# First norm's gain spread by TensorE from one row and read from PSUM, with the order of the first tiles' casts, low parts and transposes written down

## The chip, the cores and the metric

The kernel runs on one core of one Trainium2 chip. The metric is the device time of one execution in microseconds (us), as a median of runs. Five engines work side by side, each through its own list of instructions in order: TensorE (PE: matmuls and transposes, with its weight loads listed as PEld), VectorE (DVE), ScalarE (ACT), GpSimd (POOL) and SyncE (SP), which here only issues DMAs. ACT issues some DMAs too. An instruction starts when it is first in its engine's list and the semaphores it waits for have been raised.

## The reference

One layer of a hybrid encoder over 1024 positions with 1024 channels, all in float32:

```python
h = rmsnorm(x, g_mix[l])
z = h @ w_in[l]
...
y_pool = pool_mixer(u_pool, w_pool_grp[l], pool_scale[l])
...
y_attn = diff_attention(q, k, v, g_q[l], g_k[l], lam, g_sub[l], lambda_init)
gates = jax.nn.sigmoid(h @ w_gate[l] + b_gate[l])
merged = (gates[..., :D_MODEL] * (y_pool @ w_branch_pool[l])
          + gates[..., D_MODEL:] * (y_attn @ w_branch_attn[l]))
x = x + merged @ w_out[l]
h2 = rmsnorm(x, g_ffn[l])
x = x + jnp.square(jax.nn.relu(h2 @ w_up[l])) @ w_down[l]
```

The change touches the first line only: `rmsnorm` divides a row of x by the root of its mean square and multiplies it by the gain `g_mix`, one number for each channel.

## The kernel before

The 1024 positions are eight tiles t of 128 rows. For each, `norm_x(t)` calls `norm_transpose`: ACT squares the row and sums it (`Square`, with a second instruction that reads the sum out), DVE and POOL make the root `rs`, DVE multiplies x by `rs` and by the gain in two halves of 512 channels (`hn`), and PE transposes each half in four 128x128 blocks into one PSUM bank (`hps`). From the bank `split` makes two things, two blocks at a time: ACT casts a high part to the rounded type fp32r (`hT` with last index 0), and DVE subtracts that from the bank to leave a low part (index 1). Each tile so has four casts and four low parts, by pairs kp = 0 to 3 of channel blocks; two pairs share a bank. Tile 0 takes its sum of squares in two halves, on ACT and on DVE (`halves`).

The weights of a head (`rqkv`, eight blocks of 128 channels by 384 columns) are split the same way into `wqkv`, by ACT and by DVE or POOL. A product `z` of one tile and one head is `mm3` for eight blocks k: three matmuls each (high times high, high times low, low times high), 24 in all, into one of two PSUM banks. After z of a tile come the row norms of its q and k (`sq`, `ms`, `qn`), the V part, and the transposes `tk`; `qn` is read from the z bank, which is free for another tile only after that. All z of head 0 need the tiles' `hT`; the gates (`g`, with weights `fwgate`) need the `hT` too, and are filler work for PE, started by `gate_step`.

What sets the order: a scheduling layer takes the instructions in the order in which the program gives them priorities, models their times, and writes one list for each engine. `START` says in which order the first loads, splits and norms are given, `NX` in which step a tile's norm is given, `LX` in which step its x is loaded, `ORDER` how the stages of a step are interleaved. Nothing else holds one instruction behind another, except data and buffers, and a few explicit `issue_after`, the first of them at L793 for a unit of weights.

The gain is loaded by one broadcast DMA into all 128 partitions (`gmb`, 512 KB, L345), third on SP's queue behind the two halves of x0 and ahead of the eight weight loads and x1. PSUM has eight banks: two each for z, the scores (`sc`) and the transposes (`tr`), one for the output of attention (`ps_o`) and one for filler (`ps_f`). The last two are not used in the first steps.

## Time and profile before

| | us |
|---|---|
| median of 3 runs | 1529.36 (1529.09 to 1530.44) |
| the profiled execution | 1529.71 |
| its span in the trace | 1527.6 |
| TensorE busy in the span | 1509.7 |
| VectorE, ScalarE, GpSimd busy | 1048.5, 804.7, 319.8 |

The span runs from the first to the last traced instruction; 2.1 us of the profiled time lie around it. A row of a table of groups gives line, engine, operation, output and inputs, shapes and count, then busy us and mean ns, then the idle time of the engine ahead of the group and what ended it. A row of the timeline gives start, duration, engine and line, and in brackets the idle time before it with its releaser. A row of the table of waits gives the waiting engine and line, the releaser, the us in total, the number of times and the longest. The granted clock is a share of TensorE's full clock.

### The profile page before, as it was taken

What the parts mean: (1) busy time and instruction counts of PE and PEld (TensorE: products, weight loads), DVE (VectorE), ACT (ScalarE), POOL (GpSimd) and SP (SyncE); (2) the same over time, 40 slices, a digit from 0 to 9 for tenths busy, and PEclk for the clock granted to TensorE, in tenths of its full rate; (3) what the DMA queues carried; (4) which work ended last, traced back from release to release, by engine and by line L of the source; (5) the groups of instructions that cost most, each with busy time, mean ns of one, the idle gap of its engine ahead of it and who ended that gap; (6) DMA issues with size and microseconds to landing.
All of it is one profiled execution on the core that took longest, in us unless ns stands there. A gap on an engine that the chain in (4) does not pass through costs nothing.

```text
span 1527.6 us, 21675 instructions
## 1 busy us (share of the span) xinstructions
PE 1509.7 (99%) x7441; PEld 1302.0 (85%) x7441; DVE 1048.5 (69%) x2262; ACT 804.7 (53%) x1693; POOL 319.8 (21%) x412
## 2 busy tenths in 40 slices
PE   7999999999999999999999999999999999999998
PEld 6999999999898989888888888888888888888887
DVE  6776668777777777746578559766665668556572
ACT  6665556656565565454464466555555634333331
POOL 6687333335234242312100011000000000000000
PEclk9999999999999999999999999999999999999999
DMA  7253202112112131627365734554433799537750
GB/s 247 100 159 120 76 29 62 51 44 66 43 44 84 49 98 40 223 89 254 120 209 191 248 104 149 169 178 152 148 128 110 274 344 383 170 125 262 228 190 28
DMA packets 171608, 221.07 MB, mean 145 GB/s; under 512 B 10902, under 2 KB 104811, under 8 KB 171499
## 3 DMA queue, kind: packets, MB, share of 16 engines
q1 hardware_dynamic: 154090, 192.39, 38.0%
q10 hardware_dynamic: 17408, 27.30, 4.8%
q8 instruction: 59, 0.97, 0.3%
q14 instruction: 51, 0.41, 0.1%
HBM read 157.76 MB, written 61.90 MB: 144 GB/s over the span
## 4 chain that ended last, share of the span: by engine, by line
PE 95%; DVE 2%; DMA 1%; ACT 1%; SPq 1%; issue 0%; POOL 0%; DVEq 0%
PE z L126 6%; PE z L128 6%; PE z L127 6%; PE Da L126 4%; PE Da L128 4%; PE Da L127 4%; PE g L126 4%; PE g L127 4%; PE g L128 4%; PE Db L126 3%; PE Db L128 3%; PE Db L127 3%; PE X L128 3%; PE X L127 3%; PE X L126 3%; PE sc L484 2%
## 5 line engine op out<-in xcount | busy, mean ns | idle before, releaser
L126 PE MATMUL z<-wqkv,hT 128*128 128x384 f32 x512 | 174.9, 343 | 0.6 <-DVE qn L428 0.4
L128 PE MATMUL z<-wqkv,hT 128*128 128x384 f32 x512 | 173.7, 340 | 0.0
L127 PE MATMUL z<-wqkv,hT 128*128 128x384 f32 x512 | 173.5, 339 | 0.0
L495 ACT ACTIVATE s<-s,nm 128x256 f32<-128x256 f32 (+7 forms) x128 | 99.5, 778 | 46.5 <-DVE nm L487 45.6
L126 PE MATMUL g<-hT,fwgate 128*128 128x512 f32 x256 | 101.1, 395 | 0.1
L127 PE MATMUL g<-hT,fwgate 128*128 128x512 f32 x256 | 100.8, 394 | 0.0
L128 PE MATMUL g<-hT,fwgate 128*128 128x512 f32 x256 | 100.5, 393 | 0.0
L126 PEld LDWEIGHTS z<-wqkv,hT 128*128 128x128 f32 x512 | 96.8, 189 | 3.4 <-DVE qn L428 0.6
L127 PEld LDWEIGHTS z<-wqkv,hT 128*128 128x128 f32 x512 | 96.9, 189 | 3.1 <-POOL wqkv L121 0.2
L235 POOL TENSOR_TENSOR ms<-ms,mhalf 128x4 f32<-128x4 f32 x64 | 65.7, 1027 | 158.3 <-DVE ms L234 135.3
L128 PEld LDWEIGHTS z<-wqkv,hT 128*128 128x128 f32 x512 | 96.5, 189 | 2.5 <-DVE hT L121 0.3
L121 DVE TENSOR_TENSOR AT<-ta,AT 128x256 fp32r<-128x256 f32 (+1 forms) x160 | 62.2, 392 | 32.7 <-ACT AT L120 31.6
L487 DVE CUSTOM_DVE_ANT_0 s<-sc,dist 128x512 f32<-128x512 f32 (+3 forms) x128 | 73.9, 583 | 13.2 <-PE sc L485 12.1
L120 ACT CAST AT<-ta 128x256 fp32r<-128x256 f32 (+1 forms) x160 | 54.5, 347 | 37.9 <-PE ta L527 23.1
L484 PE MATMUL sc<-K,Q 128*128 128x512 f32 (+2 forms) x192 | 69.8, 365 | 0.5 <-DVE nm L487 0.5
L121 DVE TENSOR_TENSOR AS<-s,AS 128x512 fp32r<-128x512 f32 x64 | 44.1, 693 | 36.5 <-ACT AS L120 36.3
L485 PE MATMUL sc<-K,Q 128*128 128x512 f32 (+2 forms) x192 | 66.4, 350 | 0.0
L121 POOL TENSOR_TENSOR wqkv<-rqkv,wqkv 128x384 fp32r<-128x384 f32 x60 | 61.8, 1044 | 19.8 <-ACT wqkv L120 16.7
L121 POOL TENSOR_TENSOR fwgate<-frgate,fwgate 128x512 fp32r<-128x512 f32 x32 | 43.3, 1356 | 66.0 <-ACT fwgate L120 66.0
L126 PEld LDWEIGHTS g<-hT,fwgate 128*128 128x128 f32 x256 | 48.1, 188 | 9.3 <-ACT go L730 0.5
L128 PEld LDWEIGHTS g<-hT,fwgate 128*128 128x128 f32 x256 | 48.1, 188 | 8.9
L127 PEld LDWEIGHTS g<-hT,fwgate 128*128 128x128 f32 x256 | 48.1, 188 | 8.4
(455 smaller groups left out, 4485.0 us busy)
## 6 DMA issues: line engine op xcount, KB each, us to landing
wd<-in_w_down_dram SPq DMA_DIRECT2D x56, 512.0 KB, 5.6
wu<-in_w_up_dram SPq DMA_DIRECT2D x32, 512.0 KB, 4.4
udS<-us SPq DMA_DIRECT2D x64, 256.0 KB, 2.4
ur<-udS SPq DMA_DIRECT2D x32, 512.0 KB, 3.4
rqkv<-in_w_in_dram SPq DMA_DIRECT2D x64, 192.0 KB, 2.7
ud<-u ACTq DMA_DIRECT2D x48, 256.0 KB, 4.1
ur<-ud SPq DMA_DIRECT2D x24, 512.0 KB, 4.3
frgate<-in_w_gate_dram SPq DMA_DIRECT2D x32, 256.0 KB, 2.8
```

The source lines that it names most:

```text
L120: nc.scalar.copy(hi, src)
L121: return (lo_eng or nc.vector).tensor_tensor(lo, src, f(hi), op=ALU.subtract)
L126: nc.tensor.matmul(ps, lhs_hi, rhs_hi, start=first, stop=False, **kw)
L127: nc.tensor.matmul(ps, lhs_hi, rhs_lo, start=False, stop=False, **kw)
L128: nc.tensor.matmul(ps, lhs_lo, rhs_hi, start=False, stop=last, **kw)
L235: nc.gpsimd.tensor_tensor(dst, dst, mhalf[:, :n], op=ALU.pow)
L484: nc.tensor.matmul(dst, Q[:, i, 0, :], rhs, start=True, stop=False)
L485: nc.tensor.matmul(dst, Q[:, i, 1, :], rhs, start=False, stop=True)
L487: nc.vector.tensor_tensor_reduce(out=s[i][:, c : c + w], in0=sc[:, 0:w], in1=dist[:, o0 + c : o0 + c + w], scale=2.0 ** -(h + 1), scalar=B ...
L495: nc.scalar.activation(s[i][:, 0:n], s[i][:, 0:n], AF.Exp, bias=last, scale=-1.0, accum_out=Z[:, i, t : t + 1])
```

## The change

The gain comes as one row of 4 KB by a DMA on ACT's queue. PE multiplies a column of ones (one row of `ones`, so one contraction row) with each half of it, which puts the gain on all 128 partitions of two PSUM banks, those of `ps_o` and `ps_f`. The normalising products of tiles 0, 1 and 2 (`N_GP` = 3) read the gain from there; then ACT copies both banks to `gmb`, from which tiles 3 to 7 read it.

The rest is order. `in_turn` and `marks` chain a tile's casts one behind the other, and its low parts too. For tile 0 the weight splits are given between them by `split_more`, held behind the root of tile 0. The normalising product of a tile from t = 2 on is held behind the last low part of tile t-1. In z of tiles 1 to 6 the block k=4 is held behind the first half of the next tile's transposes, and k=6 behind the second. `small_params` is held behind tile 1's last low part, the first gate step behind tile 3's last cast. `START` and `NX` give tile 1's norm earlier.

```diff
--- before.py
+++ after.py
@@ -40,8 +40,8 @@
 PREP_AT = (2, 4, 6, 8)
 
 
-START = "x0 g n0 w0 w1 w2u w3u x1 s0p s1 x2 s2p s3 x3"
-NX = [-2, -1, 0, 0, 0, 1, 2, 3]
+START = "x0 g w0 w1 w2u w3u x1 n0 n1 x2 x3"
+NX = [-2, -2, 0, 0, 0, 1, 2, 3]
 LX = [-2, -2, -2, -2, 0, 0, 1, 1]
 FU = 170
 N_SC = 8
@@ -51,6 +51,7 @@
 ORDER = [(w[0], int(w[1:])) for w in O.split()]
 G_FIRST, G_Z = 9, 10
 LATE = 700
+N_GP = 3
 
 N_OP, N_E1, N_E2, N_R1, N_R2 = 8, 11, 6, 4, 3
 
@@ -115,10 +116,26 @@
     def f(ap):
         return ap.bitcast(F32)
 
+    marks = {}
+    begin = []
+
+    def in_turn(which):
+
+        behind = ExitStack()
+        if begin and which in marks:
+            behind.enter_context(tc.issue_after(marks[which]))
+        return behind
+
     def split(hi, lo, src, lo_eng=None):
 
-        nc.scalar.copy(hi, src)
-        return (lo_eng or nc.vector).tensor_tensor(lo, src, f(hi), op=ALU.subtract)
+        with in_turn("hi"):
+            marks["hi"] = nc.scalar.copy(hi, src).ins
+        if lo_eng is not None:
+            return lo_eng.tensor_tensor(lo, src, f(hi), op=ALU.subtract)
+        with in_turn("lo"):
+            lo_ins = nc.vector.tensor_tensor(lo, src, f(hi), op=ALU.subtract)
+            marks["lo"] = lo_ins.ins
+        return lo_ins
 
     def mm3(ps, lhs_hi, lhs_lo, rhs_hi, rhs_lo, first, last, more=False):
 
@@ -234,35 +251,50 @@
         nc.vector.tensor_scalar(dst, ss, c, EPS, op0=ALU.mult, op1=ALU.add)
         nc.gpsimd.tensor_tensor(dst, dst, mhalf[:, :n], op=ALU.pow)
 
-    def norm_transpose(xt, gb, t, dst, hn, small, banks, halves=False):
+    def norm_transpose(xt, gb, t, dst, hn, small, banks, halves=False, then=None):
 
         th, c0 = t // 4, (t % 4) * P
         ss = small.tile([P, 1], F32, tag="ss", name=f"ss{t}", bufs=2)
         rs = small.tile([P, 1], F32, tag="rs", name=f"rs{t}", bufs=2)
         if halves:
             s1 = small.tile([P, 1], F32, tag="ss1", name=f"ss1{t}")
-            nc.scalar.activation(hn[:, 0:512], xt[:, 0:512], AF.Square, accum_out=ss)
+            marks["hi"] = nc.scalar.activation(hn[:, 0:512], xt[:, 0:512], AF.Square, accum_out=ss).ins
             nc.vector.tensor_tensor_reduce(
                 out=hn[:, 512:D], in0=xt[:, 512:D], in1=xt[:, 512:D],
                 scale=1.0, scalar=D * EPS, op0=ALU.mult, op1=ALU.add, accum_out=s1,
             )
             nc.vector.tensor_scalar(rs, s1, ss, 1.0 / D, op0=ALU.add, op1=ALU.mult)
-            nc.gpsimd.tensor_tensor(rs, rs, mhalf[:, 0:1], op=ALU.pow)
+            marks["rs"] = nc.gpsimd.tensor_tensor(rs, rs, mhalf[:, 0:1], op=ALU.pow).ins
+            then(0)
         else:
-            nc.scalar.activation(hn, xt, AF.Square, accum_out=ss)
+            if t > 1:
+                marks.pop("hi")
+                marks.pop("lo")
+            with in_turn("hi"):
+                sq_ins = nc.scalar.activation(hn, xt, AF.Square, accum_out=ss).ins
+            if t == 1:
+                marks["hi"] = sq_ins
             rsq(rs, ss, 1, 1.0 / D)
         for j in range(2):
             js = slice(j * 512, (j + 1) * 512)
-            nc.vector.scalar_tensor_tensor(hn[:, js], xt[:, js], rs, gb[:, js], op0=ALU.mult, op1=ALU.mult)
+            with ExitStack() as behind:
+                if t >= 2:
+                    behind.enter_context(tc.issue_after(marks["hTlo", t - 1]))
+                nc.vector.scalar_tensor_tensor(hn[:, js], xt[:, js], rs, gb[j], op0=ALU.mult, op1=ALU.mult)
             trp, trtag = banks[j % len(banks)]
             ps = trp.tile([P, 512], F32, tag=trtag, name=f"hps{t}_{j}")
             for i in range(4):
                 k = 4 * j + i
-                nc.tensor.transpose(ps[:, i * P : (i + 1) * P], hn[:, k * P : (k + 1) * P], identf)
+                marks["hps", t, j] = nc.tensor.transpose(
+                    ps[:, i * P : (i + 1) * P], hn[:, k * P : (k + 1) * P], identf
+                ).ins
             for i in range(2):
                 kp = 2 * j + i
                 src = ps[:, i * 256 : (i + 1) * 256].rearrange("p (a b) -> p a b", a=2)
                 split(dst[kp, th, 0][:, :, c0 : c0 + P], dst[kp, th, 1][:, :, c0 : c0 + P], src)
+                marks["hT", t], marks["hTlo", t] = marks["hi"], marks["lo"]
+                if halves and kp in (1, 3):
+                    then(kp)
 
     def alloc_T(tile_fn, prefix, th):
         return {
@@ -313,6 +345,7 @@
             raws[h, kp] = rw
 
         def norm_x(t):
+            begin.append(t)
             if t % 4 == 0:
                 hT.update(alloc_T(htile, "hT", t // 4))
             if FU >> t & 1:
@@ -320,7 +353,12 @@
             else:
                 hn = ut([P, D], F32, f"hn{t}")
             banks = [(ps_t, "tr"), (ps_s, "sc")][: 2 if t < N_SC else 1]
-            norm_transpose(xs.pop(t), gmb, t, hT, hn, sp, banks, t == 0)
+            gb = g_ps if t < N_GP else [gmb[:, 0:512], gmb[:, 512:D]]
+            norm_transpose(xs.pop(t), gb, t, hT, hn, sp, banks, t == 0, lambda kp: split_more(kp))
+            begin.clear()
+            if t == N_GP - 1:
+                for j in range(2):
+                    nc.scalar.copy(gmb[:, j * 512 : (j + 1) * 512], g_ps[j])
 
         def split_w(h, kp, eng):
             rw = raws.pop((h, kp))
@@ -328,6 +366,11 @@
                 w = wt([P, 2, 384], f"wqkv{h}_{2 * kp + i}")
                 split(w[:, 0, :], w[:, 1, :], rw[:, i, :], eng)
                 Wh.setdefault(h, []).append(w)
+
+        def split_more(kp):
+            with tc.issue_after(marks["rs"]):
+                for p in {0: (0,), 1: (1,), 3: (2, 3)}[kp]:
+                    split_w(0, p, nc.vector if p % 2 else nc.gpsimd)
 
         KV = {}
         hT = {}
@@ -342,7 +385,11 @@
                 split_w(0, int(w[1]), nc.gpsimd if w[2:] else nc.vector)
             elif w[0] == "g":
                 gmb = ut([P, D], F32, "gmb")
-                nc.sync.dma_start(gmb, g_mix[0].partition_broadcast(P))
+                g_row = fu_tile("g_row")
+                nc.scalar.dma_start(g_row[0:1, :], g_mix)
+                g_ps = [pool.tile([P, 512], F32, tag=tag, name=f"g_ps{tag}") for pool, tag in ((ps_o, "o"), (ps_f, "f"))]
+                for j, ps in enumerate(g_ps):
+                    nc.tensor.matmul(ps, f(ones)[0:1, :], g_row[0:1, j * 512 : (j + 1) * 512], start=True, stop=True)
 
 
         rows = sp.tile([32, P], F32, name="rows")
@@ -411,7 +458,10 @@
                 l_hi = hT[k // 2, th, 0][:, k % 2, c0 : c0 + P]
                 l_lo = hT[k // 2, th, 1][:, k % 2, c0 : c0 + P]
                 w = Wh[h][k]
-                mm3(z[:, 0:384], l_hi, l_lo, w[:, 0, :], w[:, 1, :], k == 0, k == NK - 1)
+                with ExitStack() as behind:
+                    if h == 0 and 0 < t < NT - 1 and k in (4, 6):
+                        behind.enter_context(tc.issue_after(marks["hps", t + 1, k // 2 - 2]))
+                    mm3(z[:, 0:384], l_hi, l_lo, w[:, 0, :], w[:, 1, :], k == 0, k == NK - 1)
                 yield
 
         def stage_prep(h, t):
@@ -594,7 +644,8 @@
             nc.scalar.dma_start(r_dram[h].rearrange("(t q) -> t q", q=P), rT)
             yield
 
-        small_params()
+        with tc.issue_after(marks["hTlo", 1]):
+            small_params()
         N = H * NT
 
         def stage(w, g):
@@ -626,7 +677,7 @@
             for t in range(4, NT):
                 if LX[t] == g:
                     load_x(t)
-            for t in range(1, NT):
+            for t in range(2, NT):
                 if NX[t] == g:
                     norm_x(t)
             if g == G_DIST:
@@ -793,7 +844,9 @@
         with tc.issue_after(stored["lo"]):
             weight_unit(w_branch_attn, wa_dram, *units_left.pop(0))
 
-    for _ in range(G_FIRST):
+    with tc.issue_after(marks["hT", 3]):
+        gate_step()
+    for _ in range(G_FIRST - 1):
         gate_step()
     for g in range(4):
         for _ in pool_group(g):
```

Three places in the lists are spoken of in the prediction. In the rows, `hT_0_0` is a high part of tiles 0 to 3 and `hT_0_1` a low part (`hT_1_0` and `hT_1_1` for tiles 4 to 7), the number at the end of a name tells one buffer from another, and the brackets hold the semaphores that the instruction waits for, by the engine or DMA queue that raises them.

On ACT, from the first weight cast of the program to the first cast behind the transposes' second bank. Before:

```order
L120 CAST wqkv_0_200<-rqkv_0_186 128x384 [waits DMAHW3_49]
L120 CAST wqkv_1_203<-rqkv_0_186 128x384 [waits DMAHW4_49]
L120 CAST wqkv_2_206<-rqkv_1_189 128x384 [waits DMAHW5_49]
L120 CAST hT_0_0_150<-hps_0_167 128x2x128 [waits PE_49]
L120 CAST wqkv_3_209<-rqkv_1_189 128x384 [waits DMAHW6_49]
L120 CAST wqkv_4_214<-rqkv_2_192 128x384 [waits DMAHW7_49]
L120 CAST hT_0_0_154<-hps_1_177 128x2x128 [waits PE_49]
L120 CAST hT_0_0_152<-hps_0_167 128x2x128 [waits DVE_49]
```

And now:

```order
L132 CAST wqkv_0_185<-rqkv_0_155 128x384 [waits DMAHW3_49]
L132 CAST wqkv_1_188<-rqkv_0_155 128x384 [waits DMAHW4_49]
L132 CAST hT_0_0_169<-hps_0_192 128x2x128 [waits PE_49]
L132 CAST hT_0_0_171<-hps_0_192 128x2x128 [waits DVE_49]
L132 CAST wqkv_2_201<-rqkv_1_158 128x384 [waits DMAHW5_49]
L132 CAST wqkv_3_204<-rqkv_1_158 128x384 [waits DMAHW6_49]
L132 CAST hT_0_0_173<-hps_1_208 128x2x128 [waits PE_49]
L132 CAST hT_0_0_175<-hps_1_208 128x2x128 [waits DVE_49]
```

The third weight cast stood ahead of the first `hT` cast; now two weight casts stand ahead of two `hT` casts of the same bank, of which the second waits for DVE, and two more ahead of the other bank's. The weight casts of blocks 4 to 7 all stand behind.

On DVE, around the normalising product of tile 2 (`hn_278` before, `hn_283` now; tile 1's bank is `hps_0_255` and `hps_1_265` before, `hps_0_236` and `hps_1_246` now). Before:

```order
L376 SCALAR_TENSOR_TENSOR gg<-gqk 128x64 [waits DMAHW2_49,DMAHW1_49]
L379 TENSOR_TENSOR lp<-lqk 128x128 [waits DMAHW3_49]
L234 TENSOR_SCALAR ms_0_432<-ms_0_432 128x4 [waits DVE_49]
L121 TENSOR_TENSOR hT_0_1_151<-hps_0_255,hT_0_0_150 128x2x128 [waits Activation_49]
L256 SCALAR_TENSOR_TENSOR hn_278<-x_212,rs_280,gmb 128x512 [waits DMAHW4_49,Pool_49]
L256 SCALAR_TENSOR_TENSOR hn_278<-x_212,rs_280,gmb 128x512
```

And now:

```order
L136 TENSOR_TENSOR hT_0_1_170<-hps_0_236,hT_0_0_169 128x2x128 [waits Activation_49]
L251 TENSOR_SCALAR rs_313<-ss_312 128x1 [waits Activation_49]
L136 TENSOR_TENSOR hT_0_1_172<-hps_0_236,hT_0_0_171 128x2x128 [waits Activation_49]
L136 TENSOR_TENSOR hT_0_1_174<-hps_1_246,hT_0_0_173 128x2x128 [waits PE_49,Activation_49]
L136 TENSOR_TENSOR hT_0_1_176<-hps_1_246,hT_0_0_175 128x2x128 [waits Activation_49]
L423 SCALAR_TENSOR_TENSOR gg<-gqk 128x64 [waits DMAHW2_49,DMAHW1_49]
L426 TENSOR_TENSOR lp<-lqk 128x128 [waits DMAHW3_49]
L283 SCALAR_TENSOR_TENSOR hn_283<-x_255,rs_285,g_pso 128x512 [waits DMAHW4_49,Pool_49]
L283 SCALAR_TENSOR_TENSOR hn_283<-x_255,rs_285,g_psf 128x512
```

The product of tile 2 stood behind one low part of tile 1; now it stands behind all four, and behind `gg` and `lp`.

On PE, the transposes of tiles 5 and 6 (`hn_401` and `hn_467` before, `hn_408` and `hn_474` now). Before, ahead of and in z of tile 3:

```order
L126 MATMUL z_3_597<-wqkv_1_203,hT_0_0_150 128x384
L261 MATMUL hps_0_408<-identf,hn_401 128x128 [waits DVE_49,PE_49]
L261 MATMUL hps_0_408<-identf,hn_401 128x128 x3
L127 MATMUL z_3_597<-wqkv_1_203,hT_0_0_150 128x384
L261 MATMUL hps_1_418<-identf,hn_401 128x128 [waits DVE_49,PE_49]
L261 MATMUL hps_1_418<-identf,hn_401 128x128 x3
L128 MATMUL z_3_597<-wqkv_1_203,hT_0_1_151 128x384
L126 MATMUL z_3_597<-wqkv_2_206,hT_0_0_152 128x384
L261 MATMUL hps_0_474<-identf,hn_467 128x128 [waits DVE_49,PE_49,Activation_49]
L261 MATMUL hps_0_474<-identf,hn_467 128x128 x3
L127 MATMUL z_3_597<-wqkv_2_206,hT_0_0_152 128x384
```

And now, behind z of tile 3 and 22 gate products:

```order
L288 MATMUL hps_0_415<-identf,hn_408 128x128 [waits DVE_49,PE_49]
L288 MATMUL hps_0_415<-identf,hn_408 128x128 x3
L288 MATMUL hps_1_425<-identf,hn_408 128x128 [waits DVE_49,PE_49]
L288 MATMUL hps_1_425<-identf,hn_408 128x128 x3
L288 MATMUL hps_0_481<-identf,hn_474 128x128 [waits DVE_49,PE_49]
L288 MATMUL hps_0_481<-identf,hn_474 128x128 x3
L418 MATMUL cols_ps<-identf,rows 128x32 [waits DMAHW6_49,DMAHW7_49,DMAHW0_49,PE_49]
L288 MATMUL hps_1_491<-identf,hn_474 128x128 [waits DVE_49]
L288 MATMUL hps_1_491<-identf,hn_474 128x128 x3
L496 MATMUL tk_0_515<-identf,qn_0_446 128x128 [waits DVE_49]
L496 MATMUL tk_0_515<-identf,qn_0_446 128x128
L143 MATMUL z_4_671<-wqkv_0_185,hT_1_0_337 128x384 [waits DVE_49,Activation_49]
```

The transposes of both tiles lay among the products of z of tile 3, with 18 of those still behind them; now they stand behind all of them and behind each other, and z of tile 4 follows. The product `hn_474` stands on DVE behind the last low part of tile 5:

```order
L136 TENSOR_TENSOR hT_1_1_342<-hps_1_425,hT_1_0_341 128x2x128 [waits PE_49,Activation_49]
L136 TENSOR_TENSOR hT_1_1_344<-hps_1_425,hT_1_0_343 128x2x128 [waits Activation_49]
L283 SCALAR_TENSOR_TENSOR hn_474<-x_404,rs_476,gmb 128x512 [waits DMAHW6_49,Pool_49]
L283 SCALAR_TENSOR_TENSOR hn_474<-x_404,rs_476,gmb 128x512
L419 COPY cols<-cols_ps 128x24 [waits PE_49]
L420 TENSOR_SCALAR gs<-cols 128x1 [waits DVE_49]
L136 TENSOR_TENSOR hT_1_1_338<-hps_0_481,hT_1_0_337 128x2x128 [waits Activation_49]
L136 TENSOR_TENSOR hT_1_1_340<-hps_0_481,hT_1_0_339 128x2x128 [waits Activation_49]
L478 TENSOR_TENSOR qn_2_584<-z_2_525,ms_2_577 128x2x2x64 [waits PE_49,Pool_49]
```

And `qn_2`, which frees the bank for z of tile 4, stands behind two low parts of tile 6 (`hps_0_481`), where before it stood behind `cols`, with tile 6's low parts all ahead of it and taken from banks filled during z of tile 3.

## Prediction

> **What bounds the kernel now.** I read the page's busy table first, then TensorE's table of waits, then the chain that ended last.

> ```profile
> PE 1509.7 (99%) x7441; PEld 1302.0 (85%) x7441; DVE 1048.5 (69%) x2262; ACT 804.7 (53%) x1693; POOL 319.8 (21%) x412
> PE hps L261 <- DVE hn L256: 10.6, 2, 8.8
> PE X L128 <- DVE A L121: 0.9, 1, 0.9
> 8.97 5.76 DMA x<-in_x_dram
> 16.17 0.57 POOL rs L235
> 16.76 0.76 DVE hn L256
> 17.66 1.30 PE hps L261 x8
> ```

> TensorE (PE) works in 1509.7 of 1527.6 us; it is idle for 17.9. Of these, 10.6 are two waits of the first transposes for a normalised tile (8.8 before tile 0, 1.8 before tile 1); the next entry is 0.9. So nothing outside the first 19 us is to be won by a better order, but every new idle microsecond of PE is a microsecond of the result. The last four rows are the chain before tile 1: the DMA of x1, its row sum and root, the normalising product, the transposes.

> The stage table adds a cost that no table of waits counts. Its columns are the stretch, its length, busy time (with counts) of PE, weight loads, DVE, ACT and POOL, then the granted clock.

> ```profile
> 16.00:18.00 2.00, 0.34 (x3) 0.37 (x4) 1.32 (x3) 1.42 (x3) 0.56 (x1) 1.00 0.75 185
> 18.00:20.00 2.00, 2.00 (x11) 1.62 (x10) 2.00 (x9) 1.37 (x3) 1.55 (x3) 0.67 0.80 289
> 20.00:22.00 2.00, 2.00 (x9) 1.90 (x8) 1.78 (x7) 1.96 (x7) 1.92 (x3) 0.50 0.79 232
> 22.00:24.00 2.00, 2.00 (x14) 1.96 (x14) 2.00 (x7) 1.80 (x5) 1.93 (x4) 0.97 1.13 338
> ```

> After the idle time in 16 to 18, PE is busy at a clock of 0.67, 0.50 and 0.97: lost are 2 x (0.33 + 0.50 + 0.03) = 1.7 us.

> **The start.** These are timeline rows: start, duration, engine, operation, and the idle time before.

> ```profile
> 0.72 1.28 ACT L244 ACT_TABLE_LOAD   x1 [0.72 <-PEq L1514]
> 3.57 0.63 ACT L244 ACTIVATE hn<-x 128x512 f32<-128x512 f32 x1 [1.57 <-DMA x<-in_x_dram]
> 5.40 0.57 POOL L250 TENSOR_TENSOR rs<-rs,mhalf 128x1 f32<-128x1 f32 x1 [3.16 <-DVE rs L249]
> 7.95 1.41 DVE L256 SCALAR_TENSOR_TENSOR hn<-x,rs,gmb 128x512 f32<-128x512 f32 x2 [2.70 <-DMA gmb<-in_g_mix_dram]
> 8.75 1.97 PE L261 MATMUL hps<-identf,hn 128*128 128x128 f32 x8 [8.75 <-DVE hn L256]
> 9.06 5.07 POOL L121 TENSOR_TENSOR wqkv<-rqkv,wqkv 128x384 fp32r<-128x384 f32 x4 [3.08 <-DMA rqkv<-in_w_in_dram]
> 9.99 0.37 ACT L120 CAST hT<-hps 128x256 fp32r<-128x256 f32 x1
> 10.41 0.69 PE L126 MATMUL z<-wqkv,hT 128*128 128x384 f32 x1
> 12.78 0.53 ACT L120 CAST wqkv<-rqkv 128x384 fp32r<-128x384 f32 x1
> 14.75 1.06 ACT L252 ACTIVATE hn<-x 128x1024 f32<-128x1024 f32 x1 [1.44 <-DMA x<-in_x_dram]
> 15.52 0.34 PE L128 MATMUL z<-wqkv,hT 128*128 128x384 f32 x1
> 17.66 1.30 PE L261 MATMUL hps<-identf,hn 128*128 128x128 f32 x8 [1.80 <-DVE hn L256]
> 18.33 0.37 ACT L120 CAST hT<-hps 128x256 fp32r<-128x256 f32 x1 [0.85 <-PE hps L261]
> 18.75 0.69 PE L126 MATMUL z<-wqkv,hT 128*128 128x384 f32 x1
> ```

> The root for tile 0 is there at 5.97, but the product starts at 7.95, when the broadcast gain has landed. With the gain in PSUM the product can start near 6.0, 1.95 earlier, and the first z product at 10.41 - 1.95 = 8.5. What the gain costs now:

> ```profile
> gmb<-in_g_mix_dram SPq DMA_DIRECT2D x1, 512.0 KB, 6.2
> x<-in_x_dram SPq DMA_DIRECT2D x2, 256.0 KB, 3.0
> ```

> The 512 KB leave SP's queue, so the weights and x1 behind them come earlier; I take the 2 to 3 us by which a smaller load of this table lands sooner (3.0 against 6.2). The new row goes out first on ACT's queue at about 0.7, ahead of the table load, whose delay is covered: ACT sat idle for 1.57 before its first square. By the 3.0 of the x halves the row lands near 4. The two 512-column products are not in the trace. [...]

> Does z_0's end come earlier? ACT now casts w0, w1, the first two hT groups, w2, w3, two hT groups, then w4 to w7. From 8.0 (9.99 - 1.95), four hT casts of 0.37, two waits of some 0.4 for the DVE part of the same bank, and six weight casts of 0.53 end at 8.0 + 1.5 + 0.8 + 3.2 = 13.5, not before 13.31 as now (12.78 + 0.53). POOL's low part of w5 comes two of its 1.27 (5.07 over 4) after w4's cast at 11.9: 14.5, and eight products are behind it. So z_0 ends near 15.9 as now (15.52 + 0.34): the 1.95 is **not kept**. What is kept: x1 no longer sets its square (14.75). ACT is free at 13.5, so the chain from square to transposes, 17.66 - 14.75 = 2.9, ends at 16.4, with PE idle for about 0.5 instead of 1.8. z_1 starts **1.3 earlier**, and such a short gap should not bring the half clock: another **1.7**. Start: -3.0; bounds -5.0 (all of 1.95 kept too) and +3.4.

> **The new waits.** Their prices, by group (busy us, mean ns), are:

> ```profile
> L121 DVE TENSOR_TENSOR hT<-hps,hT 128x256 fp32r<-128x256 f32 x32 | 12.4, 415 | 0.3
> L120 ACT CAST hT<-hps 128x256 fp32r<-128x256 f32 x32 | 11.0, 374 | 4.3 <-PE hps L261 3.8 <-DVE hT L121 0.2
> L252 ACT ACTIVATE hn<-x 128x1024 f32<-128x1024 f32 x7 | 7.4, 1062 | 1.8 <-DMA x<-in_x_dram 1.8
> L252 ACT ACTIVATION_READ_ACCUMULATOR hn<-x 128x1 f32 x7 | 1.3, 191 | 0.0
> L730 ACT ACTIVATE go<-g,cols 128x512 f32<-128x512 f32 x2 | 1.4, 688 | 1.4 <-DVE cols L372 1.4
> L366 ACT ACTIVATE dist<-di 128x1024 f32<-128x1024 int32 x1 | 1.1, 1064 | 0.0
> L120 ACT CAST fwgate<-frgate 128x512 fp32r<-128x512 f32 x6 | 3.7, 618 | 1.0 <-DMA frgate<-in_w_gate_dram 1.0
> L423 ACT ACTIVATE sq<-z 128x256 f32<-128x256 f32 x5 | 1.9, 377 | 3.0 <-PE z L128 3.0
> L120 ACT CAST V<-z 128x128 fp32r<-128x128 f32 x5 | 1.3, 261 | 0.0
> L428 DVE TENSOR_TENSOR qn<-z,ms 128x256 f32<-128x256 f32 x5 | 2.1, 420 | 1.5 <-PE tk L446 1.3 <-POOL ms L235 0.2
> ```

> A cast is 0.37, a low part 0.42, a row square 1.06 + 0.19 = 1.25, half a normalising product 0.70 (1.41 over 2). The first cast follows the first transpose by 0.67 (18.33 - 17.66). z products at full clock go at a pitch of 0.17:

> ```profile
> 46.50 0.33 PE L128 MATMUL z<-wqkv,hT 128*128 128x384 f32 x1
> 46.67 0.33 PE L126 MATMUL z<-wqkv,hT 128*128 128x384 f32 x1
> 44.48 0.19 PEld L126 LDWEIGHTS z<-wqkv,hT 128*128 128x128 f32 x1 [0.32 <-DVE qn L428]
> ```

> *Transposes of tile 2.* The product hn2 stands on DVE behind the last low part of tile 1 (and two small products, of which I take 0.5, under a low part's 0.42 each), where before it stood behind the first. From the first transpose of tile 1: cast at 0.67 to 1.04, the square of tile 3 to 2.29, casts two and three to 3.0, the fourth behind its bank's low part to 3.9, low part 4.3, small products 4.8, hn2 5.5. PE starts z_1 at 1.1 (18.75 - 17.66), has six products, waits 0.6 for cast two (2.66) and its low part, does six more until 3.8, and reaches the transposes written in ahead of k=4: idle 1.7. Sum **+2.3**.

> *Tile 3.* Behind hn2 ACT has the first copy of the gain (by the 0.69 of a 512-column read), a square 1.25, a V cast and the first hT cast, then the other copy 0.69, dist 1.06, and three casts around sq and V of z_1: with sq 0.38 and V 0.26 each, and cast pairs that overlap a little, some 6.0 to the last cast's end, and 0.42 + 0.70 more to hn3: 7.1. PE holds 24 products at 0.17 and eight transposes at 0.14 (18.75 - 17.66 over 8) in this time, 5.2. **+1.9**, part of it before z_2's k=2, part at the transposes.

> *Gate.* The first gate step is held behind tile 3's last cast, and its weight cast (0.62) stands behind two squares (2.5) and that cast; PE comes to it 5.1 after tile 3's first transpose, the cast is done at 6.3. **+1.0** (bounds 0 and 1.3).

> *Tiles 5 and 6.* This is the largest. On PE the transposes of tile 6 now follow those of tile 5 **with nothing between**, and hn6 stands on DVE behind the last low part of tile 5; before, both lay among products of z_3, and hn6 waited for nothing of tile 5. From the first transpose of tile 5: cast until 1.04, square of tile 7 until 2.29, casts two and three until 3.0, low part 3.5, cast four 3.9, low part 4.3, hn6 5.0. PE's eight transposes take 1.1: idle **3.9**. Then z_4 waits, as in the last row above (0.32), for qn_2, since it reuses z_2's bank; but qn_2 now stands behind the low parts of tile 6, that is behind transposes (0.67), cast 0.37, go 0.69, cast 0.37, low part 0.42, qn 0.42: 2.9 after tile 6's first transpose, while PE has 1.3 of transposes. **+1.6**, less the old 0.3.

> *Clock.* A gap of 1.8 cost 1.7 above; gaps of 1.7, about 1 and 3.9 are new. I count one more drop at about half its price, since a part of the slow stretch falls into z_4's wait: +0.9; bounds 0 and three times 1.7.

> *At nothing:* the rest of the program. The same work stands there in a slightly other order up to the middle and in the same order behind it; PE's largest single wait there is the 0.9 quoted first, so I give it 0, with 2 on either side. The two copies of the gain are in the sum for tile 3; nothing else waits for them, since tile 3's product is the first to read the copy.

> **Sum.** -3.0 + 2.3 + 1.9 + 1.0 + 3.9 + 1.3 + 0.9 = +8.3 against the profiled 1529.71 (span 1527.6 and 2.1 around it): 1538.0. That run lies 0.35 above the median of 1529.36, so I say **1537.7**.

> **A rule beside it.** The row of 16 to 18 shows that 1.8 us of idle PE sufficed for a half clock of about 3.4 us. [...] By the row, all three gaps may: +5.1 in place of 0.9, 1541.9. [...]

> **Rivals.**
> - *The gain holds* (faster). The 1.95 of the start, the 1.3 at tile 1 and the 1.7 of the clock stay, and the handed-down orders cost under 2, because casts overlap (the pitch of a cast pair is under its duration) and hn6 is ready when tile 5's transposes end. 1529.4 - 5 + 2 = 1526 or down to 1524. For it: TensorE's only large waits are removed. Against: hn6 cannot start before the last low part of tile 5. It decides once the tile 6 gap is under 1. Chance 0.13.
> - *It washes out.* The start gives 4 to 5 and tile 6 costs 4, the other waits 1 or 2: 1527 to 1532. Decided by the bank waits in z_0. Chance 0.17.
> - *The gain arrives late*: the f32 row products take several microseconds, and hn starts at 8 or later. Since z_0 is tied to POOL and ACT anyway, up to 2 us are free; it gives the forecast plus 0 to 3, 1538 to 1541. Included in slower, 0.1.
> - *Clock drops at every gap*: 1542. Included in slower, 0.12.
> - The forecast and its near surroundings (1533 to 1541): 0.48.

> Faster by over 0.2% is below 1526.3, slower above 1532.4; a measurement of this kernel can tell about that much from no change. Chances: faster 0.13, same 0.17, slower 0.70. The range reaches from 1528 (leaving out the gain and a piece of the wash-out) to 1543 (the drops at every gap).

> **What would show it.** Right: hn of tile 0 near 6.0; z_0 still ending near 15.9; x1's square released by ACT's own order and not by a DMA; in TensorE's table of waits, hps <- DVE hn over 15 us in all with three or more entries, the longest after the start near 4, between 40 and 55 us; z <- DVE qn near 1.5; clock 1.00 in 18 to 22. Wrong: z_0 ending before 14.5, or no gap over 2 us between the transposes of tiles 5 and 6. After 70 us the two orders cost the same; a difference there would be a cause that I don't have.

## The result and the profile after

The changed kernel takes 1539.27 us (median of 5 runs, 1539.01 to 1540.83), the kernel before beside it 1529.56: a ratio of 1.0066 with a 95% interval of 1.0055 to 1.0078. It is **slower by 9.7 us**. The span of its profiled execution is 1537.2 us, 9.6 more than before.

These are the busy row of the page and TensorE's table of waits of the changed kernel (engine and line, releaser, us in total, times, longest):

```profile
PE 1516.6 (99%) x7445; PEld 1304.4 (85%) x7445; DVE 1047.8 (68%) x2262; ACT 807.8 (53%) x1695; POOL 318.8 (21%) x412
PE hps L288 <- DVE hn L283: 6.7, 5, 3.9
PE g_pso L392 <- DMA g_row<-in_g_mix_dram: 2.7, 1, 2.7
PE sc L534 <- DVE nm L537: 1.5, 1, 1.5
PE z L144 <- POOL wqkv L134: 1.1, 2, 0.6
PE z L143 <- ACT K L503: 0.8, 1, 0.8
PE g L143 <- ACT fwgate L132: 0.6, 1, 0.6
```

The wait of 8.8 us for the first transposes is gone from the table. Of it, 2.1 us are the earlier start (the transposes begin at 6.67 instead of 8.75); the rest is there still, as the wait of 2.7 for the gain's row and as the time in which TensorE spreads the gain. What is new is the row of 3.9 among the five of `hps`. The timeline of the changed kernel shows the start and the waits that follow:

```profile
2.73 2.04 PE L392 MATMUL g_pso<-g_row,ones 1*128 1x512 f32 x2 [2.73 <-DMA g_row<-in_g_mix_dram]
4.57 1.91 PE L392 MATMUL g_psf<-g_row,ones 1*128 1x512 f32 x2
5.87 0.75 DVE L283 SCALAR_TENSOR_TENSOR hn<-x,rs,g_pso 128x512 f32<-128x512 f32 x1 [0.76 <-POOL rs L267]
8.29 0.67 PE L143 MATMUL z<-wqkv,hT 128*128 128x384 f32 x1
15.44 0.34 PE L145 MATMUL z<-wqkv,hT 128*128 128x384 f32 x1
16.09 1.23 PE L288 MATMUL hps<-identf,hn 128*128 128x128 f32 x8 [0.31 <-DVE hn L283]
17.18 0.44 PE L143 MATMUL z<-wqkv,hT 128*128 128x384 f32 x1
21.60 0.63 PE L288 MATMUL hps<-identf,hn 128*128 128x128 f32 x4 [1.31 <-DVE hn L283]
27.88 0.63 PE L288 MATMUL hps<-identf,hn 128*128 128x128 f32 x4 [1.02 <-DVE hn L283]
33.76 0.50 PE L143 MATMUL g<-hT,fwgate 128*128 128x512 f32 x1 [0.63 <-ACT fwgate L132]
47.29 0.63 PE L288 MATMUL hps<-identf,hn 128*128 128x128 f32 x4 [3.90 <-DVE hn L283]
50.23 0.66 PE L143 MATMUL z<-wqkv,hT 128*128 128x384 f32 x1 [0.84 <-ACT K L503]
```

The first product of tile 0 starts at 8.29 instead of 10.41, but its last is issued at 15.44 against 15.52: two microseconds are lost on the way. z of tile 1 starts at 17.18, 1.57 earlier than before. By 50 us that is paid back several times. These rows show the path that the long wait follows, from the transposes of tile 5 to the normalising product of tile 6:

```profile
42.36 1.03 PE L288 MATMUL hps<-identf,hn 128*128 128x128 f32 x8
43.43 1.06 ACT L274 ACTIVATE hn<-x 128x1024 f32<-128x1024 f32 x1
45.66 0.37 ACT L132 CAST hT<-hps 128x256 fp32r<-128x256 f32 x1 [0.55 <-DVE hT L136]
46.06 0.42 DVE L136 TENSOR_TENSOR hT<-hps,hT 128x256 fp32r<-128x256 f32 x1 [0.44 <-ACT hT L132]
46.40 1.40 DVE L283 SCALAR_TENSOR_TENSOR hn<-x,rs,gmb 128x512 f32<-128x512 f32 x2
```

ACT squares tile 7 between the casts of tile 5; the last low part ends at 46.48, and `hn` of tile 6 starts with it. The stretches of two microseconds behind the long wait show the clock (third column from the end):

```profile
46.00:48.00 2.00, 0.71 (x5) 0.55 (x5) 1.75 (x3) 0.08 (x2) 0.00 (x0) 1.00 0.00 0
48.00:50.00 2.00, 1.39 (x7) 0.97 (x6) 1.34 (x5) 1.78 (x5) 0.00 (x0) 0.56 0.03 10
50.00:52.00 2.00, 1.77 (x6) 1.80 (x7) 1.94 (x6) 0.97 (x3) 0.46 (x1) 0.50 0.31 121
52.00:54.00 2.00, 2.00 (x8) 2.00 (x7) 1.49 (x3) 0.36 (x1) 0.00 (x0) 0.50 0.00 0
54.00:56.00 2.00, 2.00 (x10) 2.00 (x9) 0.00 (x0) 0.00 (x0) 0.00 (x0) 0.73 0.00 0
```

After the gap the clock is at half for some 7 us (48.25 to 55.07), in which TensorE is busy but for 0.84. Busy time times the missing share is 1.39 x 0.44 + 1.77 x 0.5 + 2 x 0.5 + 2 x 0.27 = 3.0 us.

### The profile page after: what moved, and what is told of

Same layout as the page of the kernel before. It is cut to its first block, busy times and chain, and to the rows that moved or that the text cites. A ratio compares the mean times of both kernels' runs of the same rounds, so it can differ in the third digit from the quotient of the medians.

```text
span 1537.2 us, 21688 instructions
## 1 busy us (share of the span) xinstructions
PE 1516.6 (99%) x7445; PEld 1304.4 (85%) x7445; DVE 1047.8 (68%) x2262; ACT 807.8 (53%) x1695; POOL 318.8 (21%) x412
## 4 chain that ended last, share of the span: by engine, by line
PE 91%; DVE 4%; DMA 2%; ACT 2%; issue 1%; POOL 1%; SPq 0%; ACTq 0%; DVEq 0%; POOLq 0%
PE z L143 5%; PE z L144 5%; PE z L145 5%; PE Da L143 4%; PE Da L145 4%; PE Da L144 4%; PE g L143 3%; PE g L144 3%; PE g L145 3%; PE Db L145 3%; PE Db L143 3%; PE Db L144 3%; PE X L145 3%; PE X L144 3%; PE X L143 3%; PE sc L534 2%
## 5 line engine op out<-in xcount | busy, mean ns | idle before, releaser
L252 POOL TENSOR_TENSOR ms<-ms,mhalf 128x4 f32<-128x4 f32 x64 | 66.0, 1032 | 138.6 <-DVE ms L251 134.6
L537 DVE CUSTOM_DVE_ANT_0 s<-sc,dist 128x512 f32<-128x512 f32 (+3 forms) x128 | 74.3, 584 | 14.4 <-PE sc L535 13.5
L484 POOL TENSOR_TENSOR qn<-qn,ggh 128x128 f32<-128x128 f32 x64 | 32.8, 514 | 107.6 <-DVE qn L478 82.0
## 6 DMA issues: line engine op xcount, KB each, us to landing
wd<-in_w_down_dram SPq DMA_DIRECT2D x56, 512.0 KB, 5.1
wu<-in_w_up_dram SPq DMA_DIRECT2D x32, 512.0 KB, 4.8
udS<-us SPq DMA_DIRECT2D x64, 256.0 KB, 2.3
ur<-udS SPq DMA_DIRECT2D x32, 512.0 KB, 3.5
ud<-u ACTq DMA_DIRECT2D x48, 256.0 KB, 3.8
ur<-ud SPq DMA_DIRECT2D x24, 512.0 KB, 6.7
frgate<-in_w_gate_dram SPq DMA_DIRECT2D x32, 256.0 KB, 2.6
```

The source lines that it names most:

```text
L252: nc.gpsimd.tensor_tensor(dst, dst, mhalf[:, :n], op=ALU.pow)
L484: nc.gpsimd.tensor_tensor(qn[:, :, 1, :], qn[:, :, 1, :], ggh.unsqueeze(1).broadcast_to([P, 2, HD]), op=ALU.mult)
L537: nc.vector.tensor_tensor_reduce(out=s[i][:, c : c + w], in0=sc[:, 0:w], in1=dist[:, o0 + c : o0 + c + w], scale=2.0 ** -(h + 1), scalar=B ...
```

## The experiments

My theory: the hold of a tile's normalising product behind the last low part of the tile before makes the waits, and the waits pull the clock down. The rivals: the gain itself costs (products on TensorE, copies on ACT, reads from PSUM); or the chains of casts, or the held gate step, cost. "Before" stands for the kernel before, run beside each group on the same chip.

### The gain alone

The kernel before, with the gain's row, its two products, `N_GP` = 3 and the two copies, and nothing of the order:

```diff
-                nc.sync.dma_start(gmb, g_mix[0].partition_broadcast(P))
+                g_row = fu_tile("g_row")
+                nc.scalar.dma_start(g_row[0:1, :], g_mix)
...
+                    nc.tensor.matmul(ps, f(ones)[0:1, :], g_row[0:1, j * 512 : (j + 1) * 512], start=True, stop=True)
```

> The kernel before with the gain alone: one row, two TensorE products into the banks of ps_o and ps_f, tiles 0 to 2 read it from PSUM, then two copies to gmb; no order is written down. If the loss of the change is its order (my reading), this keeps the earlier start and loses nothing big: 1526 to 1530, ratio 0.998 to 1.000, no wait of the transposes over 2 us after the start. If the PSUM gain itself costs (products on TensorE, copies on ACT, reads from PSUM), it is 1532 or more.

Measured: 1531.99, ratio 1.0020 (1.0010 to 1.0029). It falls between the two expectations, at the edge of the second: slower than before, though nothing is held. Rows of the timeline of its profiled execution (1534.29, so 2.3 over the median):

```profile
17.36 0.59 ACT L328 COPY gmb<-g_pso 128x512 f32<-128x512 f32 x1
18.19 1.08 ACT L253 ACTIVATE hn<-x 128x1024 f32<-128x1024 f32 x1
19.25 1.06 ACT L253 ACTIVATE hn<-x 128x1024 f32<-128x1024 f32 x1
20.54 0.61 ACT L328 COPY gmb<-g_psf 128x512 f32<-128x512 f32 x1
21.92 0.69 PE L127 MATMUL z<-wqkv,hT 128*128 128x384 f32 x1 [2.14 <-ACT hT L121]
```

Since x and the gain come earlier, ACT's list now has both copies and two squares between the casts of tile 1, and TensorE waits 2.14 us for a cast; the clock is at half from 21.59 to 25.00. A further wait of 3.0 us lies far behind, where `ta` waits for `s`. So an earlier start was worth nothing by itself here: the work moves, and ACT becomes the engine that is waited for. The two copies (0.59 and 0.61) belong to the gain and stand ahead of the awaited cast, so the rival that the gain itself costs is in part borne out; how much of the 2.2 us is theirs was not separated. That is why an order was worth writing down at all.

### The order alone

The changed kernel with the broadcast DMA back in its place in `START`, and the gain read from `gmb` by all tiles:

```diff
-                g_row = fu_tile("g_row")
-                nc.scalar.dma_start(g_row[0:1, :], g_mix)
...
+                nc.sync.dma_start(gmb, g_mix[0].partition_broadcast(P))
```

> The changed kernel with the gain by the broadcast DMA as before, all of the written order kept. If the order is the loss: 1538 to 1543, with the wait of 3.9 us before the transposes of tile 6 still there, and the start as late as before (first z product near 10.4). If the gain in PSUM is the loss: 1531 or less.

Measured: 1542.54, ratio 1.0088 (1.0073 to 1.0103). TensorE's waits and the row at tile 6:

```profile
PE hps L288 <- DVE hn L283: 14.9, 4, 8.9
51.15 0.63 PE L288 MATMUL hps<-identf,hn 128*128 128x128 f32 x4 [3.90 <-DVE hn L283]
```

The order makes the loss, as expected. The same 3.90 is there without any gain in PSUM, and with this order the gain in PSUM is worth 1542.54 - 1539.27 = 3.3 us.

### No hold of the normalising product

```diff
-            with ExitStack() as behind:
-                if t >= 2:
-                    behind.enter_context(tc.issue_after(marks["hTlo", t - 1]))
-                nc.vector.scalar_tensor_tensor(hn[:, js], xt[:, js], rs, gb[j], op0=ALU.mult, op1=ALU.mult)
+            nc.vector.scalar_tensor_tensor(hn[:, js], xt[:, js], rs, gb[j], op0=ALU.mult, op1=ALU.mult)
```

> The changed kernel without the hold of the normalising product of tiles 2 to 7 behind the last low part of the tile before. If that hold makes the waits before the transposes of tiles 2, 3 and 6 (1.3, 1.0 and 3.9 us) and what follows them (z of tile 4, the second half clock): 1530 to 1532, so 7 to 9 us under the changed kernel, and under 1.5 us of waits for hn after tile 1. If the chains of casts and low parts or the held gate step are the cause instead: 1536 or more.

Measured: 1529.11, ratio 0.9998 (0.9989 to 1.0008), 10.2 us under the changed kernel and 0.9 under the expected range. TensorE's waits for the transposes:

```profile
PE hps L285 <- DVE hn L280: 1.5, 2, 1.1
PE hps L285 <- DVE hT L136: 0.7, 2, 0.3
```

Two lines removed take back the whole loss. The chains of casts and the held gate step are still in; by themselves they can't be the cause. So are the blocks k=4 and k=6 of z, held behind the next tile's transposes; whether the hold of the product would cost as much without these was not tried. But the start's 1.6 us are not a gain either: they go into small waits until 35 us.

### The hold for some tiles

Four kernels hold tiles 2 to 5, 6 and 7, 4 and 5, 2 and 3; of each only the condition changes:

```diff
-                if t >= 2:
+                if 2 <= t < 6:
```

> The changed kernel with that hold for tiles 2 to 5 only; those of 6 and 7 are free. If the 3.9 us before tile 6's transposes stand alone, they go and nothing follows: 1534 to 1535. If the rival is right, that the three bursts of transposes (tiles 5, 6, 7) stand between the gates and z of tile 4 with nothing to cover them, the wait only moves, to the transposes of tile 7 and to z of tile 4 behind qn_2: 1537 to 1539.

> The changed kernel with the hold of the normalising product for tiles 6 and 7 only; 2 to 5 are free. If the hold costs by tile and adds up (all of it 10.2 us, tiles 2 to 5 alone 6.6, so 3.6 for these two): 1532 to 1533. If the 3.9 us at tile 6 arise only because the holds of 2 to 5 have used up z of tile 3 and the gates before tile 5's transposes come: those transposes lie inside z of tile 3 again, the hold finds its low parts done, and it is 1529 to 1530.5, as without any hold.

> The changed kernel with the hold for tiles 4 and 5 only. If the pile-up (transposes of tiles 5, 6 and 7 with no products left to cover them) comes from these two: 1532.5 to 1535, with a wait of over 1.5 us between 42 and 50 us. If it comes from the lateness of tiles 2 and 3: 1529 to 1531.

> The changed kernel with the hold for tiles 2 and 3 only. If these two cost only their own waits (1.3 and 1.0 us before the transposes of tiles 2 and 3, less what the kernel without any hold waits there, 0.4 to 0.9): 1530 to 1532 and no wait over 1 us behind 32 us. If they start the pile-up: 1534 or more.

| held | us | ratio to before (interval) | above no hold (1529.11) | half clock behind the start, us |
|---|---|---|---|---|
| 2 to 5 | 1535.69 | 1.0043 (1.0028 to 1.0058) | 6.6 | 3.4 |
| 6 and 7 | 1531.61 | 1.0015 (1.0006 to 1.0024) | 2.5 | 0 |
| 4 and 5 | 1537.26 | 1.0052 (1.0040 to 1.0065) | 8.2 | 10.2 |
| 2 and 3 | 1533.51 | 1.0026 (1.0017 to 1.0035) | 4.4 | 3.4 |
| 2 to 7 (the change) | 1539.27 | 1.0066 (1.0055 to 1.0078) | 10.2 | 6.8 |

The kernel before, run beside these groups, took 1529.24 to 1529.84, so the fourth column is good to about 0.6. In the kernel without any hold the clock is 1.00 in all stretches from 16 to 80 us.

The holds don't add up: 2 and 3 with 4 and 5 would make 12.6, held together they make 6.6. A part of this is the clock, which was at half for 10.2 us with 4 and 5 held and for 3.4 with 2 to 5. TensorE's busy time in these, times the missing half, is 4.5 us against 1.7, while the idle time differs little (17.9 and 18.6 us in the whole span). With 2 to 5 held, the wait of 3.9 is not there, but it has moved:

```profile
46.26 0.21 PE L418 MATMUL cols_ps<-identf,rows 32*128 32x32 f32 x1 [1.57 <-issue]
48.28 0.66 PE L496 MATMUL tk<-identf,qn 128*128 128x128 f32 x2 [1.81 <-DVE cols L419]
```

`cols_ps` takes a bank that the transposes use too. The profile names no releaser for its wait ("issue"), so that it waits for the bank to be emptied is my reading. The same pair, 1.79 and 1.82, stands in the kernel that holds 4 and 5 only. By its time, 2 to 5 held lies between the two expectations, 0.7 over the first and 1.3 under the second. By the trace the rival was nearer, since the wait only moved, though to other places than it named: three bursts of transposes with no products left between them leave TensorE idle for 3.4 us here, against 3.9 and 0.84 in the changed kernel.

With 4 and 5 held the time is 2.3 over the expected range. The pair of waits between 42 and 50 us is there as expected; what was not foreseen is a wait of 1.89 for a cast of `hT` at 29.50 and the half clock from 30.55 to 33.97 behind it, besides that from 47.62 to 54.45.

With 6 and 7 held alone the transposes of tile 6 come inside other work and there is no such wait. The time lies between its two expectations, 0.4 under the first and 1.1 over the second. Of the 2.5, the trace shows 1.3: `z <- qn` (0.7 against 0.4 without any hold), and `sc` for `nm` behind 80 us (1.4 against 0.4), where the order differs too. The rest is open.

For 2 and 3 no wait over 1 us arises between 32 and 80 us, but the time is 1.5 over the range: 1.9 us lie far behind, where `ta` waits for `s` at 90.32, and the only half clock of that kernel, from 91.52 to 94.93, follows it. Each hold so shifts the rest of the lists as well.

### The gap filled

The changed kernel with products that nothing reads, ahead of the transposes of tile 6:

```diff
+            if (t, j) == (6, 0):
+                fill_ps = ps_o.tile([P, 512], F32, tag="o", name="fill_ps")
+                with tc.issue_after(marks["hps", 5, 1]):
+                    for _ in range(18):
+                        nc.tensor.matmul(fill_ps[:, 0:384], dst[0, 0, 0][:, 0, 0:P], Wh[0][0][:, 0, :], start=True, stop=True)
```

> The changed kernel with 18 more products (tile 0's high part times the first weights, 384 columns, into the idle bank of ps_o; nothing reads them) on TensorE between the transposes of tiles 5 and 6: 3.1 us of work in the gap of 3.9. If the half clock from 48 to 55 us follows from that gap: clock 1.00 from 46 to 58, z of tile 4 takes 4.2 instead of 6.5 us, and the time is 1536 to 1538, 1.5 to 3 under the changed kernel in spite of more work. If the clock has another cause: 1539 to 1540 and the same 0.5 from 50 to 54.

And the same with `range(9)`:

> As the kernel with the gap filled, with 9 products in place of 18: 1.6 us of work right behind tile 5's transposes, so about 2.3 us of the gap stay idle. If the clock falls after any gap like the 1.8 us of the kernel before: 0.5 for 3.4 us or more between 46 and 56 us. If it takes a gap of about 3 us: 1.00 throughout. Either way 1537 to 1541, since the rest of the program stands in another order than in the changed kernel.

With 18 products the remaining wait is 0.75; stretches of that kernel:

```profile
48.00:50.00 2.00, 1.57 (x11) 1.19 (x11) 1.61 (x5) 0.89 (x2) 0.00 (x0) 1.00 0.00 0
50.00:52.00 2.00, 1.32 (x8) 1.32 (x8) 1.77 (x5) 1.60 (x6) 0.46 (x1) 1.00 0.34 131
52.00:54.00 2.00, 2.00 (x13) 2.00 (x13) 1.99 (x5) 0.58 (x2) 0.00 (x0) 1.00 0.00 0
```

With 9 products 2.31 us of the wait are left; the row and the stretches of that kernel:

```profile
47.65 0.78 PE L293 MATMUL hps<-identf,hn 128*128 128x128 f32 x4 [2.31 <-DVE hn L283]
48.00:50.00 2.00, 2.00 (x10) 1.36 (x8) 0.92 (x5) 1.32 (x3) 0.00 (x0) 0.50 0.00 0
50.00:52.00 2.00, 1.32 (x5) 1.21 (x5) 1.94 (x6) 1.48 (x4) 0.45 (x1) 0.50 0.34 131
52.00:54.00 2.00, 2.00 (x8) 2.00 (x7) 1.96 (x4) 0.00 (x0) 0.00 (x0) 0.50 0.00 0
54.00:56.00 2.00, 2.00 (x11) 2.00 (x10) 0.12 (x1) 0.36 (x1) 0.00 (x0) 0.80 0.00 0
```

Filled, z of tile 4 runs from 50.71 to 54.95 at a clock of 1.00, 4.24 us; in the changed kernel it runs from 50.23 to 56.70, 6.47. So the half clock at this place follows from the gap, and with 2.31 us of idle time it falls just as with 3.90. The times, 1539.53 (18 products; its profiled execution, with a span of 1542.4, is longer than that) and 1539.38 (9), tell nothing of this: the added products move the rest of the lists, and in the first the wait of `ta` for `s` (1.9 us) appears, with a half clock of its own from 99.96 to 103.37. The expected gain in the time did not come, the expected clock did.

### Tile 0's weight splits earlier

The kernel without the hold, and

```diff
-                for p in {0: (0,), 1: (1,), 3: (2, 3)}[kp]:
+                for p in {0: (0, 1), 1: (2,), 3: (3,)}[kp]:
```

> As the kernel without the hold, and tile 0's weight splits given earlier between its casts: pairs 0 and 1 behind the root, pair 2 behind the second cast, pair 3 behind the fourth. If z of tile 0 ends late because POOL's low parts of w4 and w5 wait for ACT's casts behind the hT casts (POOL idle 3.3 us until 11.8, TensorE waiting 0.6 and 0.5 for them): those two waits go and z of tile 0 ends 1 to 1.5 earlier, 1527.5 to 1528.5. If z of tile 0 is tied elsewhere (the cold clock, DVE): 1529 to 1530.

Measured: 1528.49, ratio 0.9998 (0.9989 to 1.0006); not to be told from before by the interval. The trace shows what was expected. POOL's low parts without and with this edit, and the transposes of tile 1 with it:

```profile
12.24 2.28 POOL L134 TENSOR_TENSOR wqkv<-rqkv,wqkv 128x384 fp32r<-128x384 f32 x2 [4.00 <-ACT wqkv L132]
...
10.18 1.98 POOL L134 TENSOR_TENSOR wqkv<-rqkv,wqkv 128x384 fp32r<-128x384 f32 x2 [2.11 <-ACT wqkv L132]
15.28 0.90 PE L285 MATMUL hps<-identf,hn 128*128 128x128 f32 x5 [1.00 <-DVE hn L280]
```

The two waits of z of tile 0 for POOL are gone, and tile 1's transposes start at 15.28 instead of 16.57. From its first to its last product z of tile 0 takes 5.54 us here (8.41 to 13.95), against 7.15 in the changed kernel and 5.11 before. So 1.6 of the start's two microseconds were lost there; for the rest, more of the first products go at the slow pitch of 0.32 (until 10.68 in the changed kernel, from 8.76; from 10.90 to 11.87 before).

### The gate step not held

The kernel without the hold of hn, and

```diff
-    with tc.issue_after(marks["hT", 3]):
-        gate_step()
-    for _ in range(G_FIRST - 1):
+    for _ in range(G_FIRST):
```

> As the kernel without the hold of hn, and the first gate step not held behind tile 3's casts. If the held gate costs by itself (0.6 us of wait for its weight cast in the changed kernel): 1528 to 1529. If the hold protects (gate weight casts on ACT would come ahead of tile 1's and 2's casts): 1530.5 to 1533.

Measured: 1539.20, ratio 1.0065 (1.0052 to 1.0077). The direction of the second theory, and much more than it gave. Its timeline:

```profile
22.33 0.62 ACT L132 CAST fwgate<-frgate 128x512 fp32r<-128x512 f32 x1 [5.76 <-DMA frgate<-in_w_gate_dram]
23.27 0.69 PE L143 MATMUL z<-wqkv,hT 128*128 128x384 f32 x1 [5.56 <-ACT hT L132]
```

The cast of the gate's weights stands ahead of tile 1's casts in ACT's list, its DMA lands at 22.3, and everything behind it on ACT waits for 5.76 us; the clock is at half from 20.07 to 26.90. The hold of the gate, which I had counted as a cost, is worth 10 us in this order.

### A version that is faster than both

No hold of hn, the weight splits early, and work given later in two places:

```diff
-NX = [-2, -2, 0, 0, 0, 1, 2, 3]
+NX = [-2, -2, 0, 0, 1, 2, 3, 4]
...
-G_DIST, G_COLS = 1, 2
+G_DIST, G_COLS = 2, 3
```

> No hold of hn, tile 0's weight splits early, and two shifts of when work is given: the norms of tiles 4 to 7 one step later, the distances on ACT and the columns one step later each. If what is left between the transposes (0.5 at 22 to 24, 0.6 at 24 to 30, 0.3 at 30 to 40 us) is ACT and DVE behind hT casts of tiles that come too soon: another 0.8 to 1.2 under the kernel with early weight splits, 1526.5 to 1528.0, under the kernel before by more than its interval. If those gaps are bound to the transposes' banks: 1528.5 to 1529.5.

Measured: **1526.12** (1525.67 to 1526.79), before 1529.24, ratio 0.9981 (0.9973 to 0.9990): faster than the kernel before by 3.1 us and than the changed kernel by 13. TensorE's largest waits after the start are now:

```profile
PE X L145 <- DVE A L134: 0.9, 1, 0.9
PE Y L143 <- DVE u L1296: 0.8, 1, 0.8
PE hps L285 <- ACT sq L470: 0.5, 1, 0.5
```

From 26 to 80 us TensorE is busy without a gap, at full clock. The time is 0.4 under the expected range. Three things are changed at once against the changed kernel, and the share of each was not separated; without the two later steps it was 1528.49.

## Why the prediction was right

1537.7 was forecast and 1539.27 measured, with the mechanism and the place that were named. By terms, predicted against the trace (us, + is slower):

| term | predicted | measured |
|---|---|---|
| start of z of tile 1 | -1.3 | -1.57 (17.18 against 18.75) |
| half clock of the kernel before gone | -1.7 | -1.7 (clock 1.00 until 46 us) |
| tile 2 | +2.3 | +1.6 (0.26 before k=2 and 1.31) |
| tile 3 | +1.9 | +1.0 |
| gate | +1.0 | +0.6 |
| tile 6 | +3.9 | +3.9 |
| z of tile 4 | +1.3 | +0.8 (0.84 less 0.08) |
| half clock after the gap | +0.9 | +3.0 |
| rest of the program | 0 | +1.4 (idle 2.48 against 1.09 from 80 to 900 us) |
| sum | +8.3 | +9.0 of 9.6 |

- *The start.* Right to within 0.3 us: hn at 5.87 (6.0), z of tile 0 ending at 15.8 (15.9), the gap at tile 1 0.31 (0.5), z of tile 1 1.57 earlier (1.3). The square of x1 starts at 12.99 (13.5) behind ACT's own casts. That POOL's low parts hold the end was shown by moving the splits.
- *The gain's products* took 2.04 and 1.91, two instructions each (x2 in the rows). The second ends near 6.5, when the second half of hn starts: they are hidden, but only just. That they cost nothing owes something to luck. The bound of +3.4 at the start needs far longer products, and no run shows such: both were done 3.75 us after the first began (2.73 to 6.48).
- *The holds.* Removing them alone brings 1529.11; the steps were right. Tiles 2 and 3 and the gate were each priced too high; two casts in a row take 0.63 and not 0.74, and the rest of the difference was not traced. For the gate my own figures gave 1.2 (6.3 less 5.1), not the 1.0 in the sum; it was 0.6. The longest wait came to the predicted 3.9, and by the predicted path: counted from 42.36, the square ends after 2.2 (2.29 predicted), the fourth cast after 3.7 (3.9), the last low part after 4.1 (4.3), and tile 6's transposes start after 4.9 (5.0).
- *z of tile 4.* I said that it waits for `qn_2` for 1.6. It waited 0.84, and the profile puts it down to the cast of K, which I had not named. The 0.32 that I took off was the idle time of the weight load; TensorE's own was 0.08 (its transposes, started at 43.80, take 0.60, and z starts at 44.48).
- *The clock* was the term that I mis-sized most: +0.9 taken at half price, 3.0 measured. A gap of 3.9 brought 6.8 us of half clock (48.25 to 55.07), twice the 3.4 of the kernel before (18.69 to 22.10), and only 0.84 of that fell into a wait. The gaps of 1.31 and 1.02 brought none, so the forecast's case of a drop at every gap did not come. Only the gap at tile 6 lowered the clock, and one drop at the full 1.7 would have been too low as well.
- *The rest* was taken as nothing and costs 1.4, mostly one wait of `sc` for `nm` (1.5). Waits of 1 to 3 us at such places come and go in the experiments; why the scheduler places them so was not traced.
- *About 0.6* of the 9.6 stays unplaced.
- *The total.* That it misses by only 1.6 us is partly luck: the clock and the rest were 3.5 too low, and tiles 2 and 3, the gate and z of tile 4 some 2.5 too high.
- *The signs.* Two of those listed for a right forecast did not come: `hps <- DVE hn` is 6.7 in all and not over 15, since most of the wait of the start is now booked to the gain's row or filled by its products; and there is no `z <- DVE qn` near 1.5.
- *The rivals.* The gain holds, or washes out: refuted for this kernel by the 3.9 us; removing the hold makes a kernel that washes out. *The gain arrives late* is refuted by hn at 5.87.

## What to carry to other kernels

Before an order is written down, follow what stands behind the held instruction through one full round: a hold of tile t+1 behind the last step of tile t turns a pipeline into a chain as soon as no other work is left between them, and the price shows where the filler runs out, not where the hold is written. Shortening the largest wait at the start was worth nothing by itself (1531.99 with the gain alone), and with the hold removed and the weight splits early it could still not be told from before (1528.49). It was worth 3 us only in the kernel that also gives later tiles' work later. A hold that looks like a cost may be what keeps a late DMA from the head of an engine's list.

## What the runs showed of the hardware

At the start the clock column shows 1.00, though products go at a pitch of 0.32 (8.76 to 10.68 in the changed kernel) against 0.17 later. What follows is about the time behind the start, with the clock read in stretches of 0.1 us.

```profile
91.53 0.66 PE L536 MATMUL ta<-identf,s 128*128 128x128 f32 x4 [2.99 <-DVE s L513]
90.00:92.00 2.00, 0.47 (x5) 0.47 (x5) 1.97 (x3) 0.00 (x0) 1.83 (x4) 1.00 0.26 75
92.00:94.00 2.00, 2.00 (x13) 1.91 (x12) 1.89 (x8) 1.42 (x4) 0.77 (x2) 1.00 0.37 132
```

With the order alone the half clock from 24.74 lasted 3.41 us, of which TensorE was idle for 0.63; in the changed kernel it lasted 6.83, and the 0.84 ahead of z of tile 4 lies in its first half. What decides whether the clock falls, and for how long, was not shown: the gap of 2.99 without a fall is longer than that of 2.31 with one.
